# A decoder layer on one core: the first two FFN blocks interleaved, the layer norm rewritten, and FFN gating issued later

## The chip, the cores and the metric

One Trainium2 chip, one core. The metric is the device time of one execution in microseconds (us), the median of the runs of a kernel.

## The reference

A hybrid decoder layer on 256 tokens of width 2048, in float32. What matters here is its second half:

```python
merged = jax.nn.sigmoid(g_rnn) * y_rnn + jax.nn.sigmoid(g_att) * y_att
x = layer_norm(DEEPNORM_ALPHA * x + jnp.einsum('btd,de->bte', merged, w_out), ln1_g, ln1_b)
u = causal_dwconv(jnp.einsum('btd,df->btf', x, w_up), ffn_conv_w, ffn_conv_b)
gate, up = jnp.split(u, [D_FF], axis=-1)
f = jnp.einsum('btf,fd->btd', jax.nn.silu(gate) * up, w_down)
x = layer_norm(DEEPNORM_ALPHA * x + f, ln2_g, ln2_b)
```

`layer_norm` takes mean and variance over the 2048 features of a token. D_FF is 5632, so `w_up` has 88 blocks of 128 columns (44 of gate, 44 of up).

## The kernel before, in words

Every float32 weight is split into a high and a low part (fp32r) and a product is made of three matmuls, or of a 512-wide one and a 256-wide one. `order` lists the weight blocks in the order of use; `load_to` (L100) issues their loads of 1 MB on SP's queue into three buffers `raw`, and `split_to` (L122) splits block i + 1 while block i is used: ScalarE casts the high half (L116), VectorE subtracts (L119), in halves s = 0 and 1 of the contraction. `spare` gives a block a buffer in another pool. Tile's scheduler sets each engine's order from the order of issue and the priorities in the code, and waits go by semaphore.

The output projection (`o`) works by columns c of 512: `token_tile` (L204) multiplies for both token halves t. For the last column the last HELD = 3 weight tiles are held by `token_tiles_held` (L212): all of t = 0 first, then all of t = 1, and after each the function `between`, here `first_norm` (L653). That makes the residual and the statistics (L627), calls `norm` (L235), and for each quarter of 512 features `turn_x1` (L632): four transposes on TensorE into PSUM, ScalarE's copy of the high part into `xt` (L638), VectorE's subtraction of the low part (L639). The result `r1` also goes to DRAM (`zd`, L657).

`norm` runs on VectorE (centre L243, scale L247) with the reciprocal root on GpSimd (L238, L239), and the last quarter on ScalarE and GpSimd (L253 to L255). `fine` (L110) splits block gate 0 in pieces of 512 and has GpSimd split up 0.

The FFN (L685) makes block gate j, then up j: `feature_block` (L161) is 16 matmuls `high` (L166) and 16 `low` (L171) over the whole contraction, and `ffn_conv` (L672) copies out of PSUM and convolves. Silu, the product (GpSimd), the cast to `fh` and the subtraction to `fl` are issued at once, behind the block (L687 to L691). The down projection (`d`) follows with the same `norm` at its end (`second_norm`, L714), which writes each quarter to `out`. `after` and `tick` (L142) are a list of functions to be issued some blocks later; the earlier stages use it.

## Time and profile before

| | |
|---|---|
| median of 3 runs | 1459.45 us (1459.37 to 1461.41) |
| the profiled execution | 1458.57 us |
| its span, first to last instruction | 1456.7 us |
| TensorE busy | 97% |
| VectorE, ScalarE, GpSimd busy | 69%, 52%, 15% |
| mean granted TensorE clock | 0.993 of full speed |

In the rows PE is TensorE, PEld its weight loads, DVE VectorE, ACT ScalarE, POOL GpSimd and SP the queue that issues the DMAs. A name like L247 is a line of the kernel, and "idle before" is the time in which an engine stood ahead of an instruction, with what ended it. Times are us from the start of the span, of the profiled execution.

### The profile page before, as it was taken

Reading aid. Unit: us, or ns where it says so; the run is one execution under the profiler, and the core shown is the slowest. Engines: PE = TensorE matmul, PEld = TensorE weight load, DVE = VectorE, ACT = ScalarE, POOL = GpSimd, SP = SyncE. Lnnn points to the kernel's source line nnn. Section 1 sums busy time; section 2 is a strip of 40 time slices with the busy share of each in tenths; the row PEclk is TensorE's granted clock in tenths of the full one; section 3 lists DMA queues with packets and bytes.
Section 4 is the critical chain, followed back from the end, with each engine's and each line's share of the span. In section 5 each row is a group of like instructions: output and inputs, shape, how many; then the busy total and the mean of one; then the engine's idle time right before and its main releaser. Section 6 shows DMA issues by size and latency. Waiting matters only on the chain.

```text
span 1456.7 us, 19941 instructions
## 1 busy us (share of the span) xinstructions
PE 1419.7 (97%) x7718; PEld 1224.7 (84%) x7718; DVE 998.8 (69%) x1510; ACT 759.3 (52%) x1092; POOL 218.4 (15%) x215
## 2 busy tenths in 40 slices
PE   7989999999999999999799999999999999999996
PEld 6868888888888888888688888888888888888885
DVE  6777766777878686765777776777776765544456
ACT  4444555657877878634345454444444444343342
POOL 3542132120000000000411111111111110000002
...
GB/s 275 161 126 203 174 145 174 173 163 189 212 175 200 171 193 174 224 258 211 145 199 179 189 188 191 183 202 175 201 177 198 181 197 277 202 200 211 183 198 87
DMA packets 42206, 275.42 MB, mean 189 GB/s; under 512 B 4576, under 2 KB 4832, under 8 KB 10240
## 3 DMA queue, kind: packets, MB, share of 16 engines
...
## 4 chain that ended last, share of the span: by engine, by line
PE 89%; DVE 4%; POOL 4%; issue 1%; DMA 1%; ACT 1%; SPq 0%; ACTq 0%; POOLq 0%; DVEq 0%
PE psb L166 42%; PE psb L171 22%; PE psd L201 5%; PE psd L199 5%; PE psd L197 5%; PE pso L199 2%; PE pso L201 2%; PE pso L197 2%; POOL sh L332 1%; POOL qf L333 1%; DVE lo L119 1%; POOL qf L331 1%; DMA cst<-in_consts 1%; ACT hi L116 0%; DMA xraw<-in_xT 0%
## 5 line engine op out<-in xcount | busy, mean ns | idle before, releaser
L119 DVE TENSOR_TENSOR lo<-raw,hi 128x1024 fp32r<-128x1024 f32 (+2 forms) x488 | 597.5, 1227 | 346.6 <-ACT hi L116 335.5
L166 PE MATMUL psb<-xt,hi 128*128 128x512 f32 (+1 forms) x2896 | 741.0, 395 | 7.5 <-ACT hi L116 5.6
L116 ACT CAST hi<-raw 128x1024 fp32r<-128x1024 f32 (+1 forms) x488 | 510.4, 1048 | 310.1 <-PE psd L201 130.5
L166 PEld LDWEIGHTS psb<-xt,hi 128*128 128x128 f32 (+1 forms) x2896 | 521.8, 189 | 102.3 <-ACT hi L116 5.6
L171 PEld LDWEIGHTS psb<-xt,lo 128*128 128x128 f32 (+1 forms) x2896 | 396.1, 191 | 29.0 <-issue 0.4
L171 PE MATMUL psb<-xt,lo 128*128 128x256 f32 (+1 forms) x2896 | 404.8, 283 | 0.0
L197 PE MATMUL psd<-hi,fh 128*128 128x512 f32 x352 | 136.9, 389 | 0.0
L201 PE MATMUL psd<-hi,fl 128*128 128x512 f32 x352 | 136.9, 389 | 0.0
L199 PE MATMUL psd<-lo,fh 128*128 128x512 f32 x352 | 136.9, 389 | 0.0
L689 POOL TENSOR_TENSOR y<-y 128x256 f32<-128x256 f32 x44 | 32.5, 739 | 402.7 <-DVE y L681 381.2
L681 DVE SCALAR_TENSOR_TENSOR y<-u,parm,y 128x255 f32<-128x255 f32 (+1 forms) x176 | 84.7, 481 | 4.0
L687 ACT ACTIVATE y<-y 128x256 f32<-128x256 f32 x44 | 18.4, 418 | 114.2 <-DVE y L681 114.2
L199 PEld LDWEIGHTS psd<-lo,fh 128*128 128x128 f32 x352 | 66.1, 188 | 13.8
L197 PEld LDWEIGHTS psd<-hi,fh 128*128 128x128 f32 x352 | 66.1, 188 | 13.7
L201 PEld LDWEIGHTS psd<-hi,fl 128*128 128x128 f32 x352 | 66.1, 188 | 13.6
L313 ACT COPY ev<-psb 128x256 f32<-128x256 f32 (+1 forms) x181 | 65.8, 363 | 1.0 <-PE psb L166 1.0
L238 POOL TENSOR_SCALAR rstd<-mv 128x1 f32<-128x1 f32 x4 | 3.1, 780 | 394.8 <-DVE mv L236 394.8
L690 ACT CAST fh<-y 128x256 fp32r<-128x256 f32 x44 | 17.9, 406 | 69.0 <-POOL y L689 67.1
L197 PE MATMUL pso<-hi,mh 128*128 128x512 f32 x128 | 49.9, 390 | 0.0
L199 PE MATMUL pso<-lo,mh 128*128 128x512 f32 x128 | 49.9, 390 | 0.0
L201 PE MATMUL pso<-hi,ml 128*128 128x512 f32 x128 | 49.8, 389 | 0.0
L691 POOL TENSOR_TENSOR fl<-y,fh 128x256 fp32r<-128x256 f32 x44 | 45.0, 1024 | 22.9 <-ACT fh L690 22.9
...
## 6 DMA issues: line engine op xcount, KB each, us to landing
raw<-in_w_blk SPq DMA_DIRECT2D x91, 1024.0 KB, 4.8
raw<-in_w_u SPq DMA_DIRECT2D x88, 1024.0 KB, 4.8
raw<-in_w_d SPq DMA_DIRECT2D x44, 1024.0 KB, 4.8
raw<-in_w_o SPq DMA_DIRECT2D x16, 1024.0 KB, 4.8
raw<-in_w_v SPq DMA_DIRECT2D x4, 1024.0 KB, 4.8
...
g<-in_lnrows SPq DMA_DIRECT2D x2, 1024.0 KB, 5.8
...
```

The source lines that it names most:

```text
L116: nc.scalar.copy(hi[:, :w], raw[:, s * w:(s + 1) * w])
L119: eng.tensor_sub(lo[:, o:o + step], raw[:, s * w + o:s * w + o + step], hi[:, o:o + step].bitcast(F32))
L166: nc.tensor.matmul(ps[:m, :], hi[:, o:o + m], src[:, k, :], start=k == 0, stop=k == KT - 1, skip_group_check=True)
L171: nc.tensor.matmul(ps[:m, T:], lo[:, o:o + m], src[:, k, :T], start=False, stop=False, skip_group_check=True)
L197: nc.tensor.matmul(ps, hi_at(k, t), hi[:, o:o + 512], start=first, stop=False, skip_group_check=True)
L199: nc.tensor.matmul(ps, hi_at(k, t), lo[:, o:o + 512], start=False, stop=False, skip_group_check=True)
L201: nc.tensor.matmul(ps, lo_at(k, t), hi[:, o:o + 512], start=False, stop=last, skip_group_check=True)
L313: nc.scalar.copy(t[:m], ps[:m, T:])
L681: nc.vector.scalar_tensor_tensor(y[:, s:], u[:, :T - s], w(tap), y[:, s:], op0=ALU.mult, op1=ALU.add)
L687: nc.scalar.activation(yg, yg, AF.Silu)
L689: nc.gpsimd.tensor_mul(yg, yg, yu)
L691: nc.gpsimd.tensor_sub(fl[:, j], yg, fh[:, j].bitcast(F32))
```

## The change

`norm` becomes a list of steps (`norm_steps`): a head, and per part centre and scale. All of it runs on VectorE, but for the power -0.5 on one number per token, which stays on GpSimd; the last quarter no longer goes through ScalarE and GpSimd. For t = 0 the transposes are not issued in the norm: two quarters are turned after the second of the three weight tiles of t = 1, two among those of t = 1. For t = 1 the first quarter is cut into two parts of 256. The pair gate 0 and up 0 is made by `feature_pair`, which alternates between the two blocks by quarters of the contraction. Gate 0 is split whole before the t = 0 pass, into a pool `ahead`; up 0 is split by VectorE in two halves that are issued among the steps of the t = 1 norm (`split_part`); `fine` is gone. Silu, product and casts are issued one and two blocks later through `after`, with three buffers `y`. The pool `p1` moves to the right side and is closed earlier.

```diff
-    fine = {("gate", 0): (512, nc.vector), ("up", 0): (256, nc.gpsimd)}
 def split_half(i, s, raw, w):
...
-        step, eng = fine.get(order[i][0], (w, nc.vector))
-        for o in range(0, w, step):
-            eng.tensor_sub(lo[:, o:o + step], raw[:, s * w + o:s * w + o + step], hi[:, o:o + step].bitcast(F32))
+        nc.vector.tensor_sub(lo[:, :w], raw[:, s * w:(s + 1) * w], hi[:, :w].bitcast(F32))
...
+    def feature_pair(keys, src):
+        both = [splits.pop(blk_at[key]) for key in keys]
+        pss = [psum.tile([P, 512], F32, tag="b", name="psb", bufs=4) for _ in keys]
+        for s in range(2):
+            for k0 in (8 * s, 8 * s + 4):
+                for ps, halves in zip(pss, both):
+                    for k in range(k0, k0 + 4):
+                        nc.tensor.matmul(ps, halves[s][0][:, k % 8 * P:(k % 8 + 1) * P], src[:, k, :],
+                                         start=k == 0, stop=k == KT - 1, skip_group_check=True)
+            for ps, halves in zip(pss, both):
+                for k in range(8 * s, 8 * s + 8):
+                    nc.tensor.matmul(ps[:, T:], halves[s][1][:, k % 8 * P:(k % 8 + 1) * P], src[:, k, :T],
+                                     start=False, stop=k == KT - 1, skip_group_check=True)
+        load_to(blk_at[keys[1]] + 1 + AHEAD_LOAD)
+        return pss
...
 def token_tiles_held(...):
+        if ahead:
+            spare[blk_at[keys[-1]] + 1] = ahead
+            split_to(blk_at[keys[-1]] + 2)
...
+    def norm_steps(r, g, b, t, cuts, done):
+        mean, rs = mv[:, t, 0:1], rstd[:, t:t + 1]
+        parts = [slice(c0, c1) for c0, c1 in zip(cuts, cuts[1:])]
+        def center(c):
+            nc.vector.scalar_tensor_tensor(r[:, c], r[:, c], mean, g[:, c], op0=ALU.subtract, op1=ALU.mult)
+        def head():
+            nc.vector.bn_aggr(mv[:, t, :], stats[:, t].rearrange("p c s -> p (c s)"))
+            nc.vector.tensor_scalar(rs, mv[:, t, 1:2], EPS, None, op0=ALU.add)
+            last = nc.gpsimd.tensor_tensor(rs, rs, mhalf, op=ALU.pow)
+            center(parts[0])
+            center(parts[1])
+            return last
+        def part(n):
+            c = parts[n]
+            if n > 1:
+                center(c)
+            last = nc.vector.scalar_tensor_tensor(r[:, c], r[:, c], rs, b[:, c], op0=ALU.mult, op1=ALU.add)
+            return last, done(c.start, c.stop)
+        return [head] + [lambda n=n: part(n) for n in range(len(parts))]
...
     def first_norm(t, n):
-        if n == HELD - 1:
+        if t == 0 and n == HELD - 1:
             residual(r1, xc, pss[t], t, 3)
-            norm(r1[:, t], g1[:, 0], g1[:, 1], t, lambda c: turn_x1(t, c))
+            norm(r1[:, t], g1[:, 0], g1[:, 1], t, QUARTERS, lambda c0, c1: ready.append((t, c0, c1)))
             nc.sync.dma_start(zd[t], r1[:, t])
+        elif t == 1 and n == HELD - 2:
+            turn_x1(*ready.pop(0))
+            turn_x1(*ready.pop(0))
+        elif t == 1 and n == HELD - 1:
+            steps = norm_steps(r1[:, t], g1[:, 0], g1[:, 1], t, (0, 256) + QUARTERS[1:], lambda *c: turn_x1(t, *c))
+            with tc.high_priority(100):
+                residual(r1, xc, pss[t], t, 3)
+                steps[0]()
+                steps[1]()
+                scaled = steps[2]()[0]
+                steps[3]()
+            with tc.issue_after(scaled.ins):
+                split_part(pair[1], 0)
+                for step in steps[4:]:
+                    turned.append(step()[1])
+                    turned.append(turn_x1(*ready.pop(0)))
+                split_part(pair[1], 1)
+            nc.sync.dma_start(zd[t], r1[:, t])
...
+    first = feature_pair(pair, x1t)
+    phn.close()
+    with tc.issue_after(turned[-1].ins):
+        split_to(blk_at["gate", 1] + 1)
...
     for j in range(NF):
-        yg = ffn_conv(("gate", j), j, "g")
-        nc.scalar.activation(yg, yg, AF.Silu)
-        yu = ffn_conv(("up", j), NF + j, "u")
-        nc.gpsimd.tensor_mul(yg, yg, yu)
-        nc.scalar.copy(fh[:, j], yg)
-        nc.gpsimd.tensor_sub(fl[:, j], yg, fh[:, j].bitcast(F32))
+        yg = ffn_conv(first[0] if j == 0 else feature_block(("gate", j), x1t), j, "g")
+        after(1, gate, yg)
+        tick()
+        yu = ffn_conv(first[1] if j == 0 else feature_block(("up", j), x1t), NF + j, "u")
+        after(1, product, yg, yu)
+        after(2, split_f, j, yg)
+        tick()
```

**TensorE, from the last projection matmuls (pso) to the FFN blocks (psb).** Before, the last 16 transposes (ptx; eight per two quarters) and then block gate 0 as one piece:

```order
L197 MATMUL pso<-hi_1_6529,mh 128x512
L199 MATMUL pso<-lo_1_6530,mh 128x512
L201 MATMUL pso<-hi_1_6529,ml 128x512
L635 MATMUL ptx<-ident,r_6040 128x128 x16
L166 MATMUL psb<-xt,hi_0_6710 128x512 x8
L171 MATMUL psb<-xt,lo_0_6711 128x256 x8
L166 MATMUL psb<-xt,hi_1_6715 128x512 x7
L171 MATMUL psb<-xt,lo_1_6716 128x256 x8
L166 MATMUL psb<-xt,hi_1_6715 128x512
```

In the change, with hi_0_6537 the first half of gate 0 and hi_0_6675 that of up 0:

```order
L225 MATMUL pso<-hi_1_6533,ml 128x512
L667 MATMUL ptx<-ident,r_6044 128x128 x4
L199 MATMUL psb<-xt,hi_0_6537 128x512 x4
L199 MATMUL psb<-xt,hi_0_6675 128x512
L667 MATMUL ptx<-ident,r_6044 128x128 x4
L199 MATMUL psb<-xt,hi_0_6675 128x512 x3
L199 MATMUL psb<-xt,hi_0_6537 128x512 x3
L667 MATMUL ptx<-ident,r_6044 128x128 x8
L199 MATMUL psb<-xt,hi_0_6537 128x512
L199 MATMUL psb<-xt,hi_0_6675 128x512 x4
L203 MATMUL psb<-xt,lo_0_6538 128x256 x8
L203 MATMUL psb<-xt,lo_0_6676 128x256 x6
```

Matmuls of both blocks now stand between the transposes; eight more transposes and the rest of the pair follow. Of t = 0, eight transposes stand ahead of the last 12 pso matmuls; before, 16 stood ahead of the last 18 and the last 11.

**VectorE, the t = 1 norm and what follows it.** Before:

```order
L630 BN_STATS stats<-r_6040 128x6
L236 BN_AGGR mv<-stats 128x2
L243 SCALAR_TENSOR_TENSOR r_6040<-r_6040,mv,g_6041 128x512 x2
L251 SCALAR_TENSOR_TENSOR nmr<-mv,rstd 128x1
L247 SCALAR_TENSOR_TENSOR r_6040<-r_6040,rstd,g_6041 128x512 x2
L243 SCALAR_TENSOR_TENSOR r_6040<-r_6040,mv,g_6041 128x512
L247 SCALAR_TENSOR_TENSOR r_6040<-r_6040,rstd,g_6041 128x512
L639 TENSOR_TENSOR xt<-ptx,xt 128x4x128 x4
```

In the change:

```order
L274 TENSOR_SCALAR rstd<-mv 128x1
L270 SCALAR_TENSOR_TENSOR r_6044<-r_6044,mv,g_6045 128x256 x2
L284 SCALAR_TENSOR_TENSOR r_6044<-r_6044,rstd,g_6045 128x256 x2
L270 SCALAR_TENSOR_TENSOR r_6044<-r_6044,mv,g_6045 128x512
L671 TENSOR_TENSOR xt<-ptx,xt 128x2x128 x2
L284 SCALAR_TENSOR_TENSOR r_6044<-r_6044,rstd,g_6045 128x512
L115 TENSOR_TENSOR lo_0_6676<-raw_6673,hi_0_6675 128x1024
L270 SCALAR_TENSOR_TENSOR r_6044<-r_6044,mv,g_6045 128x512
L671 TENSOR_TENSOR xt<-ptx,xt 128x4x128
L284 SCALAR_TENSOR_TENSOR r_6044<-r_6044,rstd,g_6045 128x512
L270 SCALAR_TENSOR_TENSOR r_6044<-r_6044,mv,g_6045 128x512
L115 TENSOR_TENSOR lo_1_6712<-raw_6673,hi_1_6711 128x1024
```

The subtractions into xt (L671) come between the norm's steps, and both halves of up 0's split (lo_0_6676, lo_1_6712) stand among them; two subtractions, the last scale and two subtractions follow.

**ScalarE in an FFN tile.** Before, the cast to fh stands ahead of the copy out of PSUM (ev) in every second tile:

```order
L116 CAST hi_1_7100<-raw_6946 128x1024
L690 CAST fh<-y 128x256
L313 COPY ev<-psb 128x256
L116 CAST hi_0_7150<-raw_6998 128x1024
L687 ACTIVATE y<-y 128x256
```

In the change it stands behind it:

```order
L114 CAST hi_1_7097<-raw_6941 128x1024
L341 COPY ev<-psb 128x256
L750 CAST fh<-y 128x256
L114 CAST hi_0_7145<-raw_6995 128x1024
L744 ACTIVATE y<-y 128x256
```

One row has changed places there; in the other tiles the order is the same, and silu and the weights' casts stand where they stood. Only at the first tile, where the pair ends, are more rows in another order.

## Rows read from the trace of the kernel before

**Rows 1.** The profile page, section 1: busy us, share of the span, instructions.

```profile
PE 1419.7 (97%) x7718; PEld 1224.7 (84%) x7718; DVE 998.8 (69%) x1510; ACT 759.3 (52%) x1092; POOL 218.4 (15%) x215
```

**Rows 2.** The list of TensorE's waits over the whole span, the first line: who waited for whom, us in total, times, longest us.

```profile
PE ptx L635 <- DVE r L247: 10.4, 4, 5.6
```

**Rows 3.** The timeline of all engines from 675 to 732 us, around the t = 1 pass of the projection: start us, us, engine, line, operation, out<-in, count, and in brackets the idle time before it with what ended it.

```profile
676.24 5.46 SPq L106 DMA_DIRECT2D raw<-in_w_u  x3
...
686.92 0.39 PE L197 MATMUL pso<-hi,mh 128*128 128x512 f32 x1
...
687.12 0.69 DVE L629 SCALAR_TENSOR_TENSOR r<-xres,pso 128x512 f32<-128x512 f32 x1 [5.78 <-PE pso L201]
...
690.78 0.39 PE L201 MATMUL pso<-hi,ml 128*128 128x512 f32 x1
...
691.63 1.32 PE L635 MATMUL ptx<-ident,r 128*128 128x128 f32 x8 [0.47 <-DVE r L247]
...
696.80 0.85 PEld L635 LDWEIGHTS ptx<-ident,r 128*128 128x128 f32 x8 [2.67 <-DVE r L247]
696.81 1.09 PE L635 MATMUL ptx<-ident,r 128*128 128x128 f32 x8 [2.23 <-DVE r L247]
```

**Rows 4.** The timeline of TensorE from 700 to 725 us, same columns.

```profile
700.03 0.39 PE L201 MATMUL pso<-hi,ml 128*128 128x512 f32 x1
706.03 1.94 PE L635 MATMUL ptx<-ident,r 128*128 128x128 f32 x8 [5.62 <-DVE r L247]
710.05 1.94 PE L635 MATMUL ptx<-ident,r 128*128 128x128 f32 x8 [2.07 <-DVE r L247]
711.64 3.76 PE L166 MATMUL psb<-xt,hi 128*128 128x512 f32 x8
...
719.04 2.23 PE L166 MATMUL psb<-xt,hi 128*128 128x512 f32 x9
...
724.63 0.63 PE L166 MATMUL psb<-xt,hi 128*128 128x512 f32 x2
```

The row of nine at 719.04 holds the last matmul of gate 0 and the first eight of up 0, so a block is counted from one such row's start to the next.

**Rows 5.** The timeline of VectorE from 699 to 714 us: the t = 1 norm.

```profile
703.18 1.42 DVE L243 SCALAR_TENSOR_TENSOR r<-r,mv,g 128x512 f32<-128x512 f32 x2
...
705.14 1.41 DVE L247 SCALAR_TENSOR_TENSOR r<-r,rstd,g 128x512 f32<-128x512 f32 x2
706.47 1.76 DVE L243 SCALAR_TENSOR_TENSOR r<-r,mv,g 128x512 f32<-128x512 f32 x1
```

**Rows 6.** Groups of instructions by line and shape from 686 to 725 us: line, engine, operation, names, shapes, count, then busy us, mean ns of one, and idle us before.

```profile
L639 DVE TENSOR_TENSOR xt<-ptx,xt 128x512 fp32r<-128x512 f32 x8 | 5.2, 680 | 0.8 <-ACT xt L638 0.8
L638 ACT CAST xt<-ptx 128x512 fp32r<-128x512 f32 x8 | 4.5, 586 | 6.2 <-PE ptx L635 6.2
L119 DVE TENSOR_TENSOR lo<-raw,hi 128x1024 fp32r<-128x1024 f32 x3 | 3.7, 1224 | 6.1 <-PE psb L171 3.4 <-ACT hi L116 2.6
L239 POOL TENSOR_TENSOR rstd<-rstd,mhalf 128x1 f32<-128x1 f32 x2 | 1.9, 932 | 0.2
L238 POOL TENSOR_SCALAR rstd<-mv 128x1 f32<-128x1 f32 x2 | 1.6, 782 | 166.6 <-DVE mv L236 166.6
L681 DVE SCALAR_TENSOR_TENSOR y<-u,parm,y 128x255 f32<-128x255 f32 x1 | 0.5, 478 | 0.0
L251 DVE SCALAR_TENSOR_TENSOR nmr<-mv,rstd 128x1 f32<-128x1 f32 x2 | 0.3, 160 | 0.9 <-POOL rstd L239 0.9
```

**Rows 7.** Stretches of the span: from:to us, length, then busy us (and count) of PE, PEld, DVE, ACT, POOL, the granted TensorE clock as a share of full speed (1.00 is 2.4 GHz, 0.50 is 1.2 GHz), DMA share, GB/s.

```profile
694.00:696.00 2.00, 0.58 (x3) 0.14 (x1) 2.00 (x2) 1.04 (x1) 2.00 (x2) 1.00 0.00 0
705.00:706.00 1.00, 0.00 (x0) 0.00 (x0) 0.93 (x3) 0.74 (x1) 0.03 (x1) 0.86 1.02 434
706.00:707.00 1.00, 0.96 (x5) 1.00 (x6) 1.00 (x2) 0.08 (x1) 0.85 (x1) 0.50 0.93 393
715.00:716.00 1.00, 1.00 (x5) 0.90 (x5) 0.00 (x0) 0.52 (x1) 0.00 (x0) 0.52 0.00 0
716.00:717.00 1.00, 1.00 (x9) 0.91 (x8) 0.25 (x1) 0.53 (x1) 0.00 (x0) 1.00 0.00 0
1449.00:1450.00 1.00, 0.00 (x0) 0.00 (x0) 1.00 (x2) 0.78 (x1) 0.14 (x1) 0.91 0.00 0
```

**Rows 8.** The timeline of all engines from 1444.4 us to the end: the last norm.

```profile
1443.58 1.67 DVE L247 SCALAR_TENSOR_TENSOR rg<-rg,rstd 128x512 f32<-128x512 f32 x1
...
1444.47 0.39 PE L201 MATMUL psd<-hi,fl 128*128 128x512 f32 x1
...
1445.17 0.68 DVE L629 SCALAR_TENSOR_TENSOR rg<-xc,psd 128x512 f32<-128x512 f32 x1
...
1446.90 1.41 DVE L243 SCALAR_TENSOR_TENSOR rg<-rg,mv 128x512 f32<-128x512 f32 x2
...
1451.96 1.63 DVE L247 SCALAR_TENSOR_TENSOR rg<-rg,rstd 128x512 f32<-128x512 f32 x1
```

**Rows 9.** The timeline of all engines from 1195 to 1225 us, in an FFN tile; the row of nine again holds the last matmul of one block and eight of the next.

```profile
1195.09 1.03 ACT L116 CAST hi<-raw 128x1024 fp32r<-128x1024 f32 x1
...
1199.50 2.23 PE L166 MATMUL psb<-xt,hi 128*128 128x512 f32 x9
```

**Rows 10.** The profile page: section 5, the cast to fh (busy us, mean ns | idle us before, releaser), and section 6, the loads of w_up (KB each, median us from issue to landing).

```profile
L690 ACT CAST fh<-y 128x256 fp32r<-128x256 f32 x44 | 17.9, 406 | 69.0 <-POOL y L689 67.1
...
raw<-in_w_u SPq DMA_DIRECT2D x88, 1024.0 KB, 4.8
```

More of the change, by code (lines that the diff above doesn't have):

```diff
@@ L182, in feature_block, with split_part @@
         return ps
+    def split_part(key, s):
+        i = blk_at[key]
+        assert i == done["split"]
+        load_to(i + 1)
+        raw, f = raws[i]
+        splits.setdefault(i, []).append(split_half(i, s, raw, f // 2))
+        if s == 1:
+            del raws[i]
+            done["split"] += 1
+    def feature_pair(keys, src):
[13 more added lines that the diff above has]
+        return pss
     def project(key, fn, src=None, m=P):
@@ L209, in hybrid_layer, with token_tiles_held @@
     HELD = 3
-    def token_tiles_held(keys, pss, k0, src, pool, between):
+    def token_tiles_held(keys, pss, k0, src, pool, between, ahead=None):
         spare[blk_at[keys[-1]]] = pool
@@ L268, in hybrid_layer @@
     ph1 = ExitStack()
[L269 removed]
+    p1 = ph1.enter_context(tc.tile_pool(name="p1", bufs=1, side="right"))
     cst = p1.tile([P, N_CONST - P], F32, name="cst")
@@ L630, in residual, with turn_x1 @@
         nc.vector.bn_stats(stats[:, t, c], y)
[L632 removed]
+    def turn_x1(t, c0, c1):
+        k0, k1 = c0 // P, c1 // P
         pt = psum.tile([P, 512], F32, tag="m", name="ptx", bufs=4)
[L634 to L639 removed]
+        for k in range(k0, k1):
+            nc.tensor.transpose(pt[:, (k - k0) * P:(k - k0 + 1) * P], r1[:, t, k * P:(k + 1) * P], ident)
+        ptv = pt[:, :c1 - c0].rearrange("p (k q) -> p k q", q=P)
+        hi = x1t[:, k0:k1, t * P:(t + 1) * P]
+        last = nc.scalar.copy(hi, ptv)
+        nc.vector.tensor_sub(x1t[:, k0:k1, T + t * P:T + (t + 1) * P], ptv, hi.bitcast(F32))
+        return last
     src = (lambda k, t: mh[:, k, t * P:(t + 1) * P], lambda k, t: ml[:, k, t * P:(t + 1) * P], KT)
@@ L683, in ffn_conv, with gate, product, split_f @@
         return y
-    for j in range(NF):
-        yg = ffn_conv(("gate", j), j, "g")
+    def gate(yg):
         nc.scalar.activation(yg, yg, AF.Silu)
-        yu = ffn_conv(("up", j), NF + j, "u")
+    def product(yg, yu):
         nc.gpsimd.tensor_mul(yg, yg, yu)
+    def split_f(j, yg):
         nc.scalar.copy(fh[:, j], yg)
         nc.gpsimd.tensor_sub(fl[:, j], yg, fh[:, j].bitcast(F32))
+    for j in range(NF):
+        yg = ffn_conv(first[0] if j == 0 else feature_block(("gate", j), x1t), j, "g")
[5 more added lines that the diff above has]
+        tick()
+    flush()
     phw.close()
```

53 lines of the change are left out of this document (14 added, 39 removed).

## The prediction

> **What bounds the kernel now.** I read the busy shares first. TensorE works 97% of the span [rows 1], so time can only come out of the 3% in which it stands, and of the tail. The list of waits says where TensorE stands: the largest entry is the transposes of x1 waiting for VectorE's norm, 10.4 us in four waits, the longest 5.6 [rows 2]. The FFN's 88 blocks have no entry there, and one block takes 724.63 - 719.04 = 5.59 us [rows 4].
>
> The timeline shows the four waits. The second pass of the output projection (t=1) starts at 686.92, and 17 matmuls later one starts at 690.78: 0.227 us each [rows 3]. Then TensorE takes transposes of the first half (t=0) into its queue and waits for VectorE twice, 0.47 and 2.23 us [rows 3]. Its last projection matmul ends at 700.03 + 0.39 = 700.42. Then 5.62 us of nothing, eight transposes, 2.07 us of nothing, eight more, and the first FFN block starts at 711.64 [rows 4]. The granted clock fell from 2.4 to 1.2 GHz at about 705.9, after 5.4 us without a matmul, and came back at about 716.0 [rows 7]; so the first block took 719.04 - 711.64 = 7.40 us where 5.59 is usual [rows 4]. Why the norm is slow: VectorE's 512-wide step takes 0.71 us when alone (two in 1.41 or 1.42), but 1.76 while GpSimd works on the same rows [rows 5].
>
> **The change, stretch by stretch.** The comparison ends where the second FFN block (up 0) ends: at 719.04 + 5.59 = 724.63 before [rows 4].
>
> 1. End of the projection. 36 matmuls of 0.227 us are 8.17 us. The t=0 transposes shrink from 16 to 8 in this pass, and stand behind 24 matmuls in place of 18. A transpose at full clock costs 0.85 / 8 = 0.106 us [rows 3]. Their data: the t=0 residual starts at 687.12 as before; residual, statistics and aggregate take 1.73 us up to the next step's start (1446.90 - 1445.17 in the tail, where nothing stands between them [rows 8]); then come the added constant (0.2), two centre steps with GpSimd's power of 0.93 [rows 6] beside them, and two scale steps: 687.12 + 1.73 + 0.2 + 1.41 + 1.41 = 691.9. TensorE wants it at 686.92 + 24 x 0.227 = 692.37: no wait, 0.5 us to spare. End of the pass: 686.92 + 8.17 + 0.85 + 0.17 = 696.1 (the 0.17 is a matmul's 0.39 less its 0.227). **-4.3 us.**
> The early split of gate 0 stands on VectorE ahead of the t=0 residual: 2 x 1.22 us [rows 6] in 5.78 us of idleness [rows 3]. Its load is the first of three issued from 676.24 on [rows 3] and lands 4.8 us later [rows 10]; with a cast of 1.05 the split ends near 684.6. Cost 0; if the load came over 2.5 us late, the residual would start later by the rest.
>
> 2. From the last projection matmul to the first FFN matmul, a pure VectorE chain: 0.05 to start, 1.73 up to the aggregate's end [rows 8], 0.2 for the constant (VectorE's 128x1 step is 0.16, GpSimd's 0.78 [rows 6]: it runs on VectorE now, so near the first; both ends kept), 0.05 + 0.93 + 0.05 for the power, two 256-wide scales at 0.48 (the row of 255 columns [rows 6]; half of 0.71 is the lower end, 0.71 the upper), a 512-wide centre 0.71, the first half-size subtraction 0.42 (0.68 for 512 [rows 6]), 0.1 to TensorE. Transposes and ScalarE's copies (0.59 for 512 [rows 6]) run beside the second scale and the centre. Sum 5.2 us, against 711.64 - 700.42 = 11.22. **-6.0 us.** First FFN matmul at 701.3.
>
> 3. From there to the end of the two blocks, before 724.63 - 711.64 = 12.99 us. The work itself is 2 x 5.59 = 11.18. New in it are 20 transposes (8 of t=0 moved here, 12 of t=1 that formerly ran in the stall): 2.12 us. And waits: after eight matmuls and four transposes (2.2 us) TensorE needs the next quarter's low part, before which VectorE runs the other half-size subtraction, a scale, half of up 0's split (which it now does in place of GpSimd), a centre and that subtraction: 0.42 + 0.71 + 1.22 + 0.71 + 0.68 = 3.7 us. That is 1.5 us of standing. The last quarter's scale comes 0.4 us late in the same way (scale, centre, 1.22 of split, two subtractions, scale: 4.7 us against 4.3 of TensorE work). Sum 11.18 + 2.12 + 1.5 + 0.4 = 15.2. **+2.2 us**, at full clock.
>
> 4. The last norm, at the end of the kernel. The last matmul ends at 1444.86, yet its residual starts at 1445.17, since VectorE is still in the t=0 norm with steps of 1.7 us [rows 8]. Now that norm is 8 steps of 0.71 and done before. From 1444.9: 1.73, constant 0.2, then eight steps of 0.71 with the power hidden behind two of them (0.93 + 0.1 against 1.41): 1444.9 + 1.73 + 0.2 + 5.64 = 1452.5, against 1451.96 + 1.63 = 1453.59 [rows 8]. The last output DMA follows the last step in both. **-1.1 us.** GpSimd no longer shares these rows; that VectorE does all four quarters costs two steps (1.41), and that they run at 0.71 gives back 2 x 1.0 and more.
>
> 5. The gating moved blocks later. TensorE is busy without a wait there, so it can give nothing. In the ScalarE order a tile's cast to fh moves one place, behind the copy out of PSUM. At the first tile it waits for both zd writes, which end long before. Cost 0, cover 3.6 us: the weights' cast at 1195.09 ends at 1196.12 and its block starts at about 1199.73 [rows 9].
>
> Sum: -4.3 - 6.0 + 2.2 - 1.1 = **-9.2 us**. The profiled execution of before took 1458.57 us (span 1456.7), so 1449.4 by this sum. The median of the three timed runs, 1459.45, is 0.9 above that execution; I put the same 0.9 on mine: **1450.3 us**.
>
> **Weighed against the Trainium skill.** The clock fell in the long pause, stayed at half through 706 to 707 though transposes kept TensorE 0.96 busy there, and came back only after 4.3 us of FFN matmuls [rows 4, 7]. In the tail it fell about 5.0 us after the last matmul [rows 7, 8]. The Trainium skill, "TensorE: Matmul & The Clock Gate", section "Part 4: PE-mode transpose", says that transposes do not count as work for the clock in the way matmuls do. The trace agrees as far as 706 to 707 goes. By that rule the four transposes in the new pause would not hold the clock up. That speaks against this change and is the first rival.
>
> **Rivals.**
> - *The clock falls in the new pause.* It is 701.3 - 696.1 = 5.2 us without a matmul, with four short transposes after 3.5 us. For: falls were seen after 5.4 and 5.0 us without one. Against: a pause of 2.23 us left it at full [rows 3, 7], and here no 5 us pass wholly idle. Price: before, the low clock lasted 716.0 - 705.9 = 10.1 us. The same stretch from 700.5 on would cost half of it, 5.05, less the 1.9 us of waits that it swallows: +3.1, so 1453.4. A longer stretch costs 0.5 us per us.
> - *Slower: ScalarE's queue in the FFN.* The cast to fh waits for GpSimd's product and stands ahead of weight casts; its waits come to 69.0 us over 44 tiles, 1.57 each [rows 10]. If the later gating lengthens them until a weight cast comes more than 3.6 us late, TensorE waits in every tile. Break-even is 9.2 / 44 = 0.21 us per tile; 0.5 us would give 1450.3 + 22 = 1472. Against: ScalarE keeps its pairs of casts in the same places but for that one row.
> - *The wait only moves.* VectorE's chain feeds TensorE piece by piece now; 0.5 us more at each of the three pieces that are on the path, in the pair, gives 1451.8. For: nothing is issued there to cover it. Against: each duration is from a row in which VectorE worked alone.
> That the change leaves the order as it was is excluded by the listings.
>
> **How the numbers follow.** Forecast at full clock, the small overrun of the chain included: 0.55. Clock falls: 0.38, and in 0.03 of that long enough to end within 0.2% of before. No change by something not seen here 0.03; the FFN's queue, slower, 0.04. The measurement of this kernel can tell about 0.2%, 2.9 us. So faster 0.55 + 0.35 = 0.90, same 0.06, slower 0.04. The range: below, the short ends of term 2 (0.3), the waits of term 3 shorter by 0.7, and the 0.9 between median and profiled execution not carried, 1448.4; above, the low clock and 1 us of it more than reckoned, 1454.4.
>
> **What would show it.** The first FFN matmul about 5 us after the last projection matmul; no wait of TensorE before the t=0 transposes; one stop of some 1.5 us a few matmuls into the pair; the gate 1 block starting about 20 us after the last projection matmul; 512-wide norm steps of 0.71 throughout; the span ending 3.1 us after VectorE's last step, as before. A granted clock of 0.50 under the pair means the first rival. I am wrong if the pair takes more than 20 us at full clock, or if TensorE waits inside the later FFN blocks.

## The result, with the profile after

The changed kernel takes **1449.61 us** (median of six runs, 1448.23 to 1451.43) against 1459.86 of the kernel before (six runs, 1458.22 to 1461.41): a ratio of 0.9932 with a 95% interval of 0.9921 to 0.9943. It is faster by 10.2 us. The forecast was 1450.3. The profiled execution took 1448.76 us, with a span of 1446.9.

TensorE's list of waits (who waited for whom, us in total, times, longest us):

```profile
PE ptx L667 <- DVE r L284: 3.3, 1, 3.3
...
PE psb L199 <- DVE xt L671: 1.1, 2, 0.7
```

The 10.4 us in four waits [rows 2] have become 3.3 in one and 1.1 in two. The timeline of TensorE from 686 to 725 us (start us, us, engine, line, operation, names, shapes, count, in brackets the idle time before it and what ended it), to be held against [rows 3, 4]:

```profile
692.68 1.04 PE L667 MATMUL ptx<-ident,r 128*128 128x128 f32 x8
...
696.07 0.39 PE L225 MATMUL pso<-hi,ml 128*128 128x512 f32 x1
699.78 1.08 PE L667 MATMUL ptx<-ident,r 128*128 128x128 f32 x4 [3.32 <-DVE r L284]
701.24 2.40 PE L199 MATMUL psb<-xt,hi 128*128 128x512 f32 x5 [0.37 <-DVE xt L671]
...
705.48 0.97 PE L199 MATMUL psb<-xt,hi 128*128 128x512 f32 x3 [0.70 <-DVE xt L671]
...
716.66 2.00 PE L162 MATMUL psb<-xt,hi 128*128 128x512 f32 x8
```

The t=0 transposes at 692.68 carry no bracket: they don't wait. The last projection matmul ends at 696.46, the first FFN matmul starts 4.78 us later, and the block after the pair (gate 1) starts at 716.66. In the pair TensorE stops once, for 0.70 us. But five matmuls of the pair take 2.40 us where four at 0.227 and a last one of 0.39 make 1.3. Stretches of the span (from:to, length, busy us of PE, PEld, DVE, ACT, POOL, then the granted clock, DMA share, GB/s) show why:

```profile
699.00:700.00 1.00, 0.22 (x2) 0.20 (x2) 0.95 (x3) 0.00 (x0) 0.20 (x1) 0.99 0.00 0
700.00:701.00 1.00, 0.86 (x4) 0.29 (x2) 1.00 (x3) 0.47 (x2) 0.00 (x0) 0.50 0.03 8
...
702.00:703.00 1.00, 1.00 (x4) 0.81 (x3) 1.00 (x2) 0.00 (x0) 0.00 (x0) 0.50 0.00 0
703.00:704.00 1.00, 1.00 (x7) 0.76 (x7) 1.00 (x2) 0.00 (x0) 0.00 (x0) 0.80 0.00 0
704.00:705.00 1.00, 0.78 (x4) 0.29 (x2) 0.45 (x2) 0.59 (x1) 0.00 (x0) 1.00 0.00 0
```

The clock did fall to 1.2 GHz, for 3.4 us (700.0 to 703.4), where it had been low for some 10 us before [rows 7]. VectorE's timeline, the t=1 norm and what follows:

```profile
696.50 0.69 DVE L660 SCALAR_TENSOR_TENSOR r<-xres,pso 128x512 f32<-128x512 f32 x1 [0.66 <-PE pso L225]
...
698.32 0.87 DVE L270 SCALAR_TENSOR_TENSOR r<-r,mv,g 128x256 f32<-128x256 f32 x2
699.24 0.88 DVE L284 SCALAR_TENSOR_TENSOR r<-r,rstd,g 128x256 f32<-128x256 f32 x2
...
702.30 1.22 DVE L115 TENSOR_TENSOR lo<-raw,hi 128x1024 fp32r<-128x1024 f32 x1
703.44 0.74 DVE L270 SCALAR_TENSOR_TENSOR r<-r,mv,g 128x512 f32<-128x512 f32 x1
704.73 0.69 DVE L671 TENSOR_TENSOR xt<-ptx,xt 128x512 fp32r<-128x512 f32 x1 [0.55 <-ACT xt L670]
```

All 512-wide steps take 0.69 to 0.75; the 1.76 of [rows 5] is gone. At 704.73 VectorE itself has waited, 0.55 us for ScalarE's cast. The end of the kernel, against [rows 8], and the row of the page for the cast to fh, against [rows 10]:

```profile
1436.28 0.39 PE L225 MATMUL psd<-hi,fl 128*128 128x512 f32 x1
1436.70 0.69 DVE L660 SCALAR_TENSOR_TENSOR rg<-xc,psd 128x512 f32<-128x512 f32 x1 [0.95 <-PE psd L225]
...
1442.49 1.41 DVE L284 SCALAR_TENSOR_TENSOR rg<-rg,rstd 128x512 f32<-128x512 f32 x2
```

```profile
L750 ACT CAST fh<-y 128x256 fp32r<-128x256 f32 x44 | 17.9, 407 | 70.4 <-POOL y L747 70.3
```

The last residual starts 0.03 us behind the last matmul instead of 0.31, and the span ends 10.23 us behind that matmul instead of 11.84.

So the span from the t=0 residual on falls into five stretches that can be read in every profile: from the start of that residual to the end of the last projection matmul (*pass*), to the first FFN matmul (*pause*), to the first matmul of gate 1 (*pair*), to the last matmul, and to the end. *The three* is the sum of pass, pause and pair, which is the transition. TensorE's work ahead of the t=0 residual is the same in all kernels here, though that residual starts anywhere from 687.1 to 689.2 us, 687.44 and 688.82 in two profiles of the changed kernel. A good part of the scatter of whole runs is made there, so the differences below are read from the stretches. (Before, the row at 724.63 [rows 4] still holds the last matmul of up 0, so gate 1 starts at 724.86.) The last column is how long the granted clock was low at the transition, from its stretches. The experiments are told in the next section; in the two kernels called t=0 first the first FFN matmul follows the projection directly, so they have no pause of this kind.

| kernel | pass | pause | pair | the three | gate 1 to last matmul | to the end | clock low |
|---|---|---|---|---|---|---|---|
| before | 13.30 | 11.22 | 13.22 | 37.74 | 720.00 | 11.84 | 10.2 |
| changed | 9.02 | 4.78 | 15.42 | 29.22 | 720.01 | 10.23 | 3.4 |
| changed, again | 9.03 | 4.92 | 15.95 | 29.90 | 720.00 | 10.28 | 6.8 |
| gating back | 9.03 | 4.92 | 16.11 | 30.06 | 720.01 | 10.26 | 6.8 |
| norm only | 10.52 | 9.33 | 13.93 | 33.78 | 720.00 | 10.22 | 10.2 |
| serial | 9.02 | 4.93 | 20.02 | 33.97 | 720.01 | 10.28 | 10.2 |
| fill | 9.02 | 4.72 | 14.65 | 28.39 | 720.00 | 10.23 | 0 |
| fill, transposes | 9.02 | 4.72 | 14.67 | 28.41 | 720.00 | 10.30 | 0 |
| fill, half early | 9.02 | 4.71 | 14.26 | 27.99 | 720.00 | 10.30 | 0 |
| no early split | 9.03 | 4.70 | 16.50 | 30.23 | 720.00 | 10.27 | 3.4 |
| split on GpSimd | 9.02 | 7.06 | 16.26 | 32.34 | 720.00 | 10.23 | 10.2 |
| old norm, t=0 | 9.02 | 5.47 | 16.15 | 30.64 | 720.00 | 10.29 | 6.8 |
| t=0 first | 9.04 | - | - | 28.78 | 720.00 | 10.27 | 0 |
| t=0 first, low early | 9.03 | - | - | 28.24 | 720.00 | 10.31 | 3.4 |

Of the 9.8 us between the two spans, 8.5 lie in the transition, 1.6 in the tail and 0 in the 720 us between; the residual's later start (687.44 against 687.12) takes 0.3 back.

### The profile page after: what moved, and what is told of

It is laid out like the page before. It is cut to its first block, busy times and chain, and to the rows that moved or that the text cites. A ratio compares the mean times of both kernels' runs of the same rounds, so it can differ in the third digit from the quotient of the medians.

```text
span 1446.9 us, 19922 instructions
## 1 busy us (share of the span) xinstructions
PE 1418.7 (98%) x7718; PEld 1223.4 (85%) x7718; DVE 997.9 (69%) x1521; ACT 754.0 (52%) x1089; POOL 192.9 (13%) x195
## 4 chain that ended last, share of the span: by engine, by line
PE 90%; POOL 3%; DVE 3%; issue 1%; DMA 1%; ACT 1%; SPq 0%; DVEq 0%; ACTq 0%; POOLq 0%
PE psb L162 42%; PE psb L167 21%; PE psd L221 6%; PE psd L225 6%; PE psd L223 6%; PE pso L223 2%; PE pso L221 2%; PE pso L225 2%; POOL sh L360 1%; POOL qf L361 1%; POOL qf L359 1%; DVE lo L115 1%; DMA cst<-in_consts 1%; PE psv L223 1%; PE psb L199 1%
## 5 line engine op out<-in xcount | busy, mean ns | idle before, releaser
L115 DVE TENSOR_TENSOR lo<-raw,hi 128x1024 fp32r<-128x1024 f32 (+1 forms) x488 | 598.5, 1229 | 339.1 <-ACT hi L114 331.4
L162 PE MATMUL psb<-xt,hi 128*128 128x512 f32 (+1 forms) x2864 | 731.9, 394 | 6.8 <-ACT hi L114 5.6
L162 PEld LDWEIGHTS psb<-xt,hi 128*128 128x128 f32 (+1 forms) x2864 | 515.5, 189 | 100.5 <-ACT hi L114 5.6
L167 PEld LDWEIGHTS psb<-xt,lo 128*128 128x128 f32 (+1 forms) x2864 | 391.4, 190 | 28.6 <-issue 0.3
L167 PE MATMUL psb<-xt,lo 128*128 128x256 f32 (+1 forms) x2864 | 400.2, 283 | 0.0
L275 POOL TENSOR_TENSOR rstd<-rstd,mhalf 128x1 f32<-128x1 f32 x4 | 3.7, 926 | 407.7 <-DVE rstd L274 407.7
L750 ACT CAST fh<-y 128x256 fp32r<-128x256 f32 x44 | 17.9, 407 | 70.4 <-POOL y L747 70.3
```

Of the source, the lines that this page charges most:

```text
L115: nc.vector.tensor_sub(lo[:, :w], raw[:, s * w:(s + 1) * w], hi[:, :w].bitcast(F32))
L162: nc.tensor.matmul(ps[:m, :], hi[:, o:o + m], src[:, k, :], start=k == 0, stop=k == KT - 1, skip_group_check=True)
L167: nc.tensor.matmul(ps[:m, T:], lo[:, o:o + m], src[:, k, :T], start=False, stop=False, skip_group_check=True)
```

## The experiments

**Gating back.** The changed kernel with the gating issued at once, and with two buffers `y` again:

```
-        after(1, gate, yg)
-        tick()
+        gate(yg)
...
-        after(1, product, yg, yu)
-        after(2, split_f, j, yg)
-        tick()
+        product(yg, yu)
+        split_f(j, yg)
```

> The changed kernel with the FFN's gating (silu, product, cast to fh and its rest) issued at once again, as before the change. Theory (the gating gives nothing, TensorE never waits in the FFN): the same as the changed kernel within its scatter, 1449.6 us, and the stretch from the first to the last FFN block as long as in the changed kernel within 0.3 us. Rival (later gating keeps ScalarE's queue free and is part of the gain): 2 us slower or more, and TensorE waits appear in the FFN blocks.

Measured: 1450.45 us (ratio to before 0.9941, 0.9929 to 0.9954); gate 1 to the last matmul 720.01 us, as in the changed kernel and 0.01 from before. So no wait of an FFN block has come in. The gating is worth nothing that can be seen here; the theory held. The profile brought something else: the same TensorE row at the transition as in the changed kernel, and the clock low for 6.8 us instead of 3.4.

**Norm only.** The kernel before with the new norm for both norms, nothing else:

```
...
+            nc.vector.tensor_scalar(rs, mv[:, t, 1:2], EPS, None, op0=ALU.add)
+            last = nc.gpsimd.tensor_tensor(rs, rs, mhalf, op=ALU.pow)
...
-            norm(r1[:, t], g1[:, 0], g1[:, 1], t, lambda c: turn_x1(t, c))
+            norm(r1[:, t], g1[:, 0], g1[:, 1], t, QUARTERS, lambda c0, c1: turn_x1(t, c0 // 512))
...
```

> The kernel before with the new norm alone (no work on GpSimd's or ScalarE's side but the power), in both norms; the output projection's end, the transposes, the early weights and the first FFN blocks as before. Theory (the gain is made of a shorter VectorE chain plus the overlap of transposes and two blocks): tail -1.6 us as in the changed kernel; t=0 transposes still wait some 1.5 us in the second pass (-1.5 to -2); the last projection matmul to the first FFN matmul shrinks from 11.2 to about 7 us; in all -5 to -6.5 against the kernel before, so 3 to 4.5 us slower than the changed kernel. Rival A (GpSimd sharing the rows was the whole trouble): -9 to -10, the same as the changed kernel. Rival B (the gain is the interleaving): only the tail's -1.6.

Measured: 1453.87 us (0.9968, 0.9955 to 0.9980), 5.2 below before. TensorE's timeline:

```profile
705.35 1.94 PE L637 MATMUL ptx<-ident,r 128*128 128x128 f32 x8 [6.83 <-DVE r L258]
707.85 1.22 PE L166 MATMUL psb<-xt,hi 128*128 128x512 f32 x2 [0.56 <-DVE xt L641]
```

VectorE's timeline ahead of the t=1 residual (the row at 700.29):

```profile
696.80 2.36 DVE L119 TENSOR_TENSOR lo<-raw,hi 128x512 fp32r<-128x512 f32 x2
699.09 1.27 DVE L641 TENSOR_TENSOR xt<-ptx,xt 128x512 fp32r<-128x512 f32 x2
700.29 0.67 DVE L631 SCALAR_TENSOR_TENSOR r<-xres,pso 128x512 f32<-128x512 f32 x1
```

The norm by itself gives 2.8 us of the pass, 1.9 of the pause and the 1.6 of the tail, and the pair loses 0.7. Both rivals fall: it is neither the whole nor the tail alone. What is left, 4.6 us at the transition, belongs to the rest of the change: the moved transposes, gate 0's early split, the two 256-wide first steps, the pair, and a low clock of 3.4 us instead of 10.2. The pause came to 9.3 us where I had about 7: the t=1 residual starts 1.8 us behind its matmul (700.29 against 698.52), because VectorE's row still holds two pieces of gate 0's split (2.36 us, beside GpSimd's split of up 0) and two subtractions of t=0. Two more pieces of that split stand inside the t=1 statistics (700.88 and 702.19).

**Serial.** The changed kernel with gate 0 and up 0 one after the other; `issue_after` holds up 0's matmuls back until gate 0's are issued:

```
...
+        with tc.issue_after(last.ins) if first else ExitStack():
...
+                    last = nc.tensor.matmul(ps[:, T:], halves[s][1][:, k % 8 * P:(k % 8 + 1) * P], x1t[:, k, :T],
...
```

> The changed kernel with the two first FFN blocks one after the other on TensorE: all of gate 0, then all of up 0 (each by halves, 8 high and 8 low). Theory (the pair gives TensorE work while VectorE prepares the next quarter): TensorE waits three times inside gate 0, gate 1 starts 3 to 3.5 us later than in the changed kernel, 1453 us. Rival (the chain of VectorE up to the first matmul is all that counts): no difference over 0.5 us at gate 1.

Measured: 1454.01 us (0.9967, 0.9955 to 0.9980); the pair takes 20.02 us. TensorE's list of waits has one more entry of size:

```profile
PE psb L727 <- DVE xt L671: 3.5, 4, 1.4
```

The first of the four, 0.50 us, ends the pause and has its like in the changed kernel (0.37); the other three, 1.40, 0.24 and 1.32, stand inside gate 0, as expected. The clock was low for 10.2 us. The three stretches take 4.1 us more than the changed kernel with 6.8 us of low clock, 4.75 more than with 3.4. The pair side by side is worth 4 to 5 us, somewhat more than I had expected. The waits inside gate 0 come to 3.0 us, and the rest goes with the longer low clock; that the waits lengthened it is not shown, since in the changed kernel it comes out at 3.4 and 6.8 us without them.

**Fill.** Twelve matmuls whose result nothing uses, right behind the last projection matmul:

```
+    FILL = 12
...
+            idle = psum.tile([P, 512], F32, tag="m", name="idle", bufs=4)
+            for _ in range(FILL):
+                nc.tensor.matmul(idle, mh[:, 0, :P], mh[:, 0:2, :], start=True, stop=True, skip_group_check=True)
```

> The changed kernel with 12 extra matmuls of 512 columns (0.227 us each, 2.7 us in all; their result is used by nothing) right behind the last projection matmul, in the pause in which TensorE waits for VectorE. Both theories expect the granted clock to stay at 1.0 in that stretch. Theory (VectorE's chain sets the pace there, and the low clock mostly eats waiting): the first FFN matmul at the same place, gate 1 starts 0.5 us earlier. Rival (the low clock lies on the path with half its 3.4 us): gate 1 starts 1.7 us earlier. The median moves by less than it scatters in either case, so the trace decides.

Measured: 1448.77 us (0.9931, 0.9917 to 0.9944). TensorE's timeline:

```profile
697.14 2.88 PE L703 MATMUL idle<-mh 128*128 128x512 f32 x12
700.62 0.90 PE L667 MATMUL ptx<-ident,r 128*128 128x128 f32 x4 [0.60 <-DVE r L284]
702.02 1.44 PE L199 MATMUL psb<-xt,hi 128*128 128x512 f32 x5 [0.50 <-DVE xt L671]
...
705.50 0.96 PE L199 MATMUL psb<-xt,hi 128*128 128x512 f32 x3 [0.91 <-DVE xt L671]
```

The clock stayed at 1.00 and the three stretches came to 28.39: the low clock costs 0.83 us where it lasts 3.4 us, 1.51 and 1.67 where it lasts 6.8. Both theories missed, one below and one above: a part of the slow work is hidden by the wait behind it, which grows from 0.70 to 0.91.

**Split on GpSimd.** The changed kernel with up 0's low half subtracted on GpSimd in 256-wide pieces, as before:

```
-        nc.vector.tensor_sub(lo[:, :w], raw[:, s * w:(s + 1) * w], hi[:, :w].bitcast(F32))
+        eng = nc.gpsimd if order[i][0] == ("up", 0) else nc.vector
+        step = 256 if order[i][0] == ("up", 0) else w
...
```

> The changed kernel with the low halves of up 0's split on GpSimd again, in 256-wide pieces, as before the change. Theory (VectorE must have the rows to itself): VectorE's 512-wide steps in the pair grow beyond 0.74 us wherever GpSimd works, and the start of gate 1, counted from the t=0 residual (29.2 us in the changed kernel), comes 1 to 2 us later. Rival (what counts is how much stands in VectorE's row: 2.4 us taken out of it): it comes 1 us earlier.

Measured: 1452.31 us (0.9950, 0.9937 to 0.9964), 32.34 us in the three stretches. GpSimd's and VectorE's timelines:

```profile
691.17 8.41 POOL L118 TENSOR_TENSOR lo<-raw,hi 128x256 fp32r<-128x256 f32 x8
```

```profile
690.05 1.41 DVE L273 SCALAR_TENSOR_TENSOR r<-r,mv,g 128x512 f32<-128x512 f32 x2
691.37 2.38 DVE L287 SCALAR_TENSOR_TENSOR r<-r,rstd,g 128x512 f32<-128x512 f32 x2
693.67 2.37 DVE L273 SCALAR_TENSOR_TENSOR r<-r,mv,g 128x512 f32<-128x512 f32 x2
695.96 2.35 DVE L287 SCALAR_TENSOR_TENSOR r<-r,rstd,g 128x512 f32<-128x512 f32 x2
```

The theory held in kind, with the place wrong: the pieces ran during the t=0 norm, not in the pair. Two steps of VectorE take 1.41 us up to the moment GpSimd starts and 2.35 to 2.38 from then on, so the t=1 residual starts 2.2 us late (699.43, where its matmul ended at 697.25) and the pause grows by as much. Gate 1 comes 3.1 and 2.4 us later than in the changed kernel's two profiles, where I had 1 to 2; the clock was low for 10.2 us here.

**No early split.** Gate 0 split inside the t=1 norm, ahead of up 0:

```
             with tc.issue_after(scaled.ins):
+                split_part(pair[0], 0)
+                split_part(pair[0], 1)
                 split_part(pair[1], 0)
...
```

> The changed kernel with gate 0 not split early, but on VectorE behind the first scale step of the t=1 norm, ahead of up 0's. Theory (VectorE's row sets the pace from the last projection matmul on): its two steps of 1.22 us go into the row, and gate 1 starts 2.4 us later counted from the t=0 residual. Rival (TensorE's own work and the low clock set the pace in the pair): under 1 us later.

Measured: 1451.08 us (0.9942, 0.9929 to 0.9956); the three stretches 30.23, 1.0 above the changed kernel at the same 3.4 us of low clock. I expected 2.4 and put "under 1 us" to the rival, so the result stands at the rival's edge: more than half of the 2.35 us added to VectorE's row was absorbed. At this low clock VectorE's row doesn't set the pace of the pair alone.

**Fill, and half of up 0 early.** The fill kernel with up 0's first half split ahead of the t=0 residual as well:

```
...
             split_to(blk_at[keys[-1]] + 2)
+            spare[blk_at[keys[-1]] + 2] = ahead
+            split_part(("up", 0), 0)
+            del spare[blk_at[keys[-1]] + 2]
...
-                split_part(pair[1], 0)
```

> The changed kernel with the 12 extra matmuls in the pause (result used by nothing), and besides up 0's first half split early too, in VectorE's idle time ahead of the t=0 residual. Theory (VectorE's row sets the pace in the pair, 1.22 us of it in front of the second quarter's low part): with 12 extra matmuls alone gate 1 starts 28.4 us behind the t=0 residual and TensorE waits 0.91 us there; now the wait falls to 0.3 or less, and gate 1 starts 0.6 us earlier still. Rival (the round trip transposes, ScalarE's cast, subtraction is what TensorE waits for): no earlier than with the 12 matmuls alone.

Measured: 1448.64 us (0.9924, 0.9912 to 0.9937); 27.99 us, 0.40 earlier than the fill alone. Between theory and rival again: the 0.91 us wait in front of the second quarter's matmuls is gone, but the next transposes now wait 0.61 for VectorE's scale step.

**Fill with transposes.** The fill kernel with 26 transposes instead of the twelve matmuls:

```
+    FILL = 26
...
+            for n in range(FILL):
+                nc.tensor.transpose(idle[:, n % 4 * P:(n % 4 + 1) * P], r1[:, 0, n % 8 * P:(n % 8 + 1) * P], ident)
```

> The changed kernel with 26 extra transposes (0.106 us each, 2.8 us in all; result used by nothing) in the pause, in place of the 12 extra matmuls of another run, which held the granted clock at 1.0. If transposes hold the clock as matmuls do: 1.0 throughout and gate 1 28.4 us behind the t=0 residual. If they don't: 0.50 from about 5 us behind the last projection matmul on, and gate 1 29.2 to 30.1 us behind it, as in the changed kernel's two profiles of that stretch.

Measured: 1448.50 us (0.9922, 0.9907 to 0.9938), 28.41 us. TensorE's timeline, and two stretches with the clock:

```profile
696.86 3.00 PE L703 MATMUL idle<-ident,r 128*128 128x128 f32 x26
```

```profile
700.00:701.00 1.00, 0.61 (x4) 0.40 (x4) 1.00 (x3) 0.19 (x1) 0.00 (x0) 1.00 0.02 8
701.00:702.00 1.00, 0.50 (x3) 0.27 (x2) 1.00 (x3) 0.56 (x2) 0.00 (x0) 1.00 0.00 0
```

In this profile the clock stayed at 1.00 beside transposes as it had beside matmuls.

**Old norm for t=0.** The changed kernel with the norm of before in t=0 of the first norm:

```
...
-            norm(r1[:, t], g1[:, 0], g1[:, 1], t, QUARTERS, lambda c0, c1: ready.append((t, c0, c1)))
+            norm_old(r1[:, t], g1[:, 0], g1[:, 1], t, lambda c: ready.append((t, 512 * c, 512 * c + 512)))
```

> The changed kernel with the norm of before (GpSimd and ScalarE take the last quarter) for t=0 of the first norm alone; t=1 and the second norm as changed. Theory (the t=0 transposes no longer wait because only the first two quarters are wanted in that pass and 24 matmuls stand ahead of them; GpSimd's share costs only what it delays VectorE's next work): the t=0 transposes wait under 0.5 us, VectorE's steps of 1.7 us end 0.8 us too late for the t=1 residual, and gate 1 starts 0.8 to 1 us later counted from the t=0 residual. Rival (the norm without GpSimd is what freed the t=0 transposes): they wait 2 us or more and gate 1 starts 3 to 4 us later.

Measured: 1450.97 us (0.9941, 0.9926 to 0.9957). TensorE's and VectorE's timelines:

```profile
693.51 1.04 PE L698 MATMUL ptx<-ident,r 128*128 128x128 f32 x8
```

```profile
691.97 1.41 DVE L306 SCALAR_TENSOR_TENSOR r<-r,rstd,g 128x512 f32<-128x512 f32 x2
...
695.10 1.67 DVE L306 SCALAR_TENSOR_TENSOR r<-r,rstd,g 128x512 f32<-128x512 f32 x1
696.69 1.28 DVE L702 TENSOR_TENSOR xt<-ptx,xt 128x512 fp32r<-128x512 f32 x2
697.88 0.67 DVE L691 SCALAR_TENSOR_TENSOR r<-xres,pso 128x512 f32<-128x512 f32 x1
```

The t=0 transposes don't wait even with the old norm, and the pass is the same 9.02: their place (eight, behind 24 matmuls) is enough to free them, by 0.13 us (the second scale step ends at 693.38). The old norm costs 0.6 us in the pause, through the late t=1 residual (697.88, its matmul ended at 697.29), and gate 1 comes 0.6 to 0.7 us later than in the profiles with the same 6.8 us of low clock, where I had 0.8 to 1. The rival fell.

**The columns of t=0 first.** Useful work in the pause: the 256 columns of t=0 (their high and low parts) are multiplied for both blocks as soon as they are there, those of t=1 behind; half of up 0 early:

```
...
+            token_part(first, both, 0, 0, 0, 8, x1t)
...
+    token_part(first, both, 1, 0, 0, 4, x1t)
+    token_part(first, both, 0, 1, 8, 16, x1t)
+    token_part(first, both, 1, 0, 4, 8, x1t)
+    low_part(first, both, 0, x1t)
...
```

> The changed kernel with useful work in the pause: the columns of t=0 (256 of 512) of both first blocks are multiplied as soon as their quarters of the contraction are there, 16 matmuls of 0.12 us right behind the last projection matmul and 16 more as VectorE delivers, the columns of t=1 after that; up 0's first half split early as well. Theory (from the last projection matmul on VectorE's row is the longest chain, some 13 us with all its subtractions, and TensorE work moved in front of it is saved up to that bound): the clock holds, gate 1 starts 26 us behind the t=0 residual (25.5 to 27; changed kernel 29.2, with the clock held and half of up 0 early 28.0), some 3 us faster than the changed kernel. Rival (256-column matmuls in two pieces take longer than 0.13 us each, or VectorE's added subtractions come ahead of the first piece of t=1): under 1 us faster.

Measured: 1449.98 us (0.9936, 0.9924 to 0.9949), 28.78 us. The theory failed. TensorE's timeline:

```profile
697.92 2.03 PE L197 MATMUL psb<-xt,hi 128*128 128x256 f32 x16
...
706.53 0.97 PE L197 MATMUL psb<-xt,hi 128*128 128x256 f32 x6 [1.56 <-DVE xt L672]
...
710.19 2.15 PE L197 MATMUL psb<-xt,hi 128*128 128x256 f32 x16 [1.14 <-DVE xt L672]
```

The matmuls are as fast as hoped (0.12 us each) and the clock held, but two new waits came, with 2 us of ready work (the low parts of the first half) behind them in the row. The gain, 0.4 and 1.1 us against the changed kernel's two profiles, is about what the rival named, but neither of its reasons is seen: the first subtractions of t=1 start 4.2 us behind the t=1 residual (702.32 and 698.12), 4.3 in the changed kernel.

**The changed kernel again**, as it is.

> The changed kernel once more, unchanged, on the same chip as the run with t=0's columns first. Theory (the stretch of low clock is as long as chance has it, 3.4 us in one profile and 6.5 in another of the same stretch): again at 0.50 for 3 to 7 us from about 4 to 5 us behind the last projection matmul, gate 1 29.2 to 30.1 us behind the t=0 residual, 1449.6 us within 1. Rival (the low clock of 3.4 us belongs to this kernel's order): 3.4 us and 29.2 us again, within 0.2.

Measured: 1449.95 us (0.9935, 0.9922 to 0.9947), 29.90 us, the clock low from 700.4 to 707.3. The theory held: the same kernel gives 3.4 and 6.8 us.

**The columns of t=0 first, low parts early.** The same matmuls in another order of the program:

```
...
+                low_part(first, both, 0, 0, 4, x1t)
+                token_part(first, both, 1, 0, 0, 4, x1t)
...
+                low_part(first, both, 0, 4, 8, x1t)
```

> The run with t=0's columns first, with TensorE's row in another order: the low parts of the weights (ready as soon as ScalarE's casts are) and the last transposes of t=0 stand ahead of the parts that wait for VectorE's subtractions, where they stood behind; up 0's second subtraction is VectorE's last but two. Theory (that run missed because 4 us of ready work stood behind the waits of 1.56 and 1.14 us in TensorE's row, so its row and VectorE's ran one after the other): those two waits fall under 0.6 us each, gate 1 starts 25 us behind the t=0 residual (24.5 to 26; 28.8 there, 29.2 and 29.9 in the changed kernel's two profiles), about 1445.5 us, 4 us below the changed kernel. Rival (VectorE's row with t=0's two subtractions in it is too long whatever TensorE does): 28 us or more.

Measured: 1448.72 us (1446.28 to 1449.90; 0.9920, 0.9906 to 0.9934), 28.24 us. Missed by 3 us (and the 4 us of ready work in its theory were 2). TensorE's timeline:

```profile
702.10 2.00 PE L203 MATMUL psb<-xt,lo 128*128 128x256 f32 x8
703.90 1.88 PE L197 MATMUL psb<-xt,hi 128*128 128x256 f32 x8
...
708.28 2.13 PE L197 MATMUL psb<-xt,hi 128*128 128x256 f32 x16
710.25 1.04 PE L668 MATMUL ptx<-ident,r 128*128 128x128 f32 x8
712.25 2.16 PE L197 MATMUL psb<-xt,hi 128*128 128x256 f32 x16 [0.96 <-DVE xt L672]
```

The low clock came back (702.2 to 705.6) and made the first two rows 1.7 us longer (2.00 and 1.88 against 1.10 at full clock). The last transposes stood behind sixteen matmuls, 1.4 us after VectorE had their data (its last scale ends at 708.82), and 4.8 us of matmuls were left behind their subtractions. So TensorE's own row put the round trip late; the rival's reason, VectorE's length, isn't shown. Two of the five runs took 1446.28 and 1446.53 us, 2.2 below the next; neither is the profiled one, so it stays open whether the clock held in them.

Four variants (both fills, half early, low early) have medians of 1448.50 to 1448.77, about 1 us below the changed kernel. Their intervals overlap its own, so a faster kernel is shown by the stretches alone (27.99 to 28.41 against 29.22 to 30.06), not by the times. No run takes the two 256-wide first steps out by themselves, so their share is not known.

## Why the prediction was right, point by point

1. **End of the projection, -4.3.** Measured 13.30 to 9.02, -4.28. No wait, as reckoned. The reason given was only half right: I let the uncontended norm finish the two quarters in time, but with the old norm they are in time as well, by 0.13 us, so the place of the eight transposes is enough. In the old place the new norm alone brings 2.8 of the 4.3, and 0.85 of what is left there is the work of the eight transposes that the change moves into the pair.

   The early split of gate 0 cost nothing, as forecast: the t=0 residual still has 2.72 us of idle time in front of it.
2. **The pause, -6.0.** Measured 11.22 to 4.78, -6.44. The chain was 5.2 us in the sum and is 4.78: VectorE's steps follow each other faster than their durations add. From the start of the two 256-wide scale steps to the next step it is 0.79 where I had 0.96; from the aggregate's end to the first centre step 0.1, with the constant between, where I had 0.2; and the power, 0.72 on GpSimd beside the centre steps, takes 0.92 with what surrounds it, where I had 1.03.
3. **The pair, +2.2.** Measured 13.22 to 15.42, +2.20. The number is right and its make-up wrong; that they meet is luck. (My 12.99 for before left out the last matmul of up 0, 0.23 us; for the changed pair I had 15.2.) At full clock the pair takes 14.65 (fill), with one wait of 0.91 after its first pieces and none at the last quarter, where I had 1.5 and 0.4, and 13.74 of work where I had 13.3. The other 0.77 is the low clock, which my forecast did not contain. So 15.2 is 1.0 too much for waits, 0.4 too little for work and 0.8 too little for the clock.

   VectorE's timeline in the fill, at full clock, to the subtraction that ends the wait of 0.91:

```profile
701.54 0.84 DVE L671 TENSOR_TENSOR xt<-ptx,xt 128x256 fp32r<-128x256 f32 x2
702.30 0.74 DVE L284 SCALAR_TENSOR_TENSOR r<-r,rstd,g 128x512 f32<-128x512 f32 x1
702.96 1.22 DVE L115 TENSOR_TENSOR lo<-raw,hi 128x1024 fp32r<-128x1024 f32 x1
704.10 0.75 DVE L270 SCALAR_TENSOR_TENSOR r<-r,mv,g 128x512 f32<-128x512 f32 x1
704.76 0.68 DVE L671 TENSOR_TENSOR xt<-ptx,xt 128x512 fp32r<-128x512 f32 x1
```

   There VectorE has no gap, so at full clock its row is what TensorE waits for at that place, as I had reckoned, and only the sizes were off: 3.48 us from the first half-size subtraction's end (701.96) to that subtraction's where I had 3.7, and 2.57 for TensorE's pieces where I had 2.2. At the low clock it is otherwise: the transposes come later, and VectorE itself stands 0.55 us for ScalarE's cast in front of the same subtraction (704.73 in the changed kernel). Then the wait is in part a round trip in TensorE's own row: transposes, cast, subtraction, matmul. Adding 2.35 us to VectorE's row cost 1.0 at the low clock; taking 1.2 out at full clock gave 0.4, with a new wait of 0.61 for the same row further on.
4. **The tail, -1.1.** Measured -1.61. From the last matmul to the end of VectorE's last step it is 7.23 us, where I had 7.6: again a pair of steps is followed by the next 1.32 to 1.33 us after its start, where I had 1.41. The end then comes 3.0 us later, not 3.1.
5. **The gating, 0.** Measured 0.01; the casts to fh wait 70.4 us over 44 tiles (69.0 before).

The sum was -9.2; the spans differ by 9.8, because the pause gave 0.4 and the tail 0.5 more than reckoned, less the 0.3 of the later residual.

**The rivals.** *The clock falls in the new pause*, chance 0.38, was the one that took place: in all seven profiles of kernels with an empty pause of 4.7 us or more at this place (changed, again, gating back, serial, no early split, split on GpSimd, old norm), and in norm only and before too. "Empty" means with nothing but the four transposes. The step that failed was the argument against it: falls "seen after 5.4 and 5.0 us", so that 5.2 us with four transposes in it would often pass. It fell 3.5 us behind the last matmul in the changed kernel's first profile and 2.6 in its second. The price was too high in its turn: 3.1 us for 10.1 us of low clock, where it lasted 3.4 or 6.8 and cost 0.8 to 1.7. Its time of 1453.4 was therefore wrong. The forecast "at full clock" lay close by luck: the clock was not full, but its own waits were 1.0 us too long. *ScalarE's queue* didn't happen. *The wait only moves* didn't either: one stop of 0.70 and the first piece's 0.37, not three of 0.5 above the sum.

The rule weighed in the prediction is that transposes don't count as work for the clock in the way matmuls do (the Trainium skill, "TensorE: Matmul & The Clock Gate", section "Part 4: PE-mode transpose"). The run with 26 transposes in the pause doesn't bear it out, as the clock stayed at 1.00. That is one profile. The mean granted clock of whole runs points the same way: 0.995 to 0.997 in the four runs of that kernel and 0.996 to 0.997 in the ten with twelve matmuls in the pause, against 0.993 to 0.995 in eleven runs of the changed kernel; it also holds low stretches elsewhere, so it settles no single run. Nor does work in the pause always go with a full clock: the two kernels with t=0 first, whose TensorE rows are alike up to 702 us, show 1.00 in one profile and a fall in the other.
